# Layer norm with a residual add: 8-row tiles against 4-row tiles, with more and smaller buffers

## Chip, cores, metric

The kernel runs on one core of one Trainium2 chip. The metric is the device time of one execution in microseconds (us). The "span" of a profile is the profiled execution itself; it is about 2 us shorter than the device time (272.0 against 273.9 us in the profiled run of the kernel before).

## The reference

```python
# x, residual: (16, 1024, 512) float32; gamma, beta: (512,)
z = x + residual
mean = np.mean(z, axis=-1, keepdims=True)
var = np.var(z, axis=-1, keepdims=True)
return gamma * ((z - mean) / np.sqrt(var + eps)) + beta     # float32
```

There are 16,384 rows of 512 values. Each of the 128 partitions holds 128 consecutive rows, so "a row" below means one row on each of 128 partitions (256 KiB of each tensor), and there are 128 of them.

## The kernel before

The rows are cut into tiles: 14 of 8 rows, then 8 of 2 rows (the tail).

```python
R_MAIN = 8; R_TAIL = 2
n_tail = 2 * (R_MAIN // R_TAIL)
...
    R = R_MAIN if rem > n_tail * R_TAIL else R_TAIL
...
xz    = tile_pool(name="xz", bufs=3)      # x, later z       8 rows f32 each
rl    = tile_pool(name="rl", bufs=3)      # residual         8 rows f32 each
mids  = tile_pool(name="mids", bufs=2)    # ut, wt           8 rows bf16 each
outs  = tile_pool(name="outs", bufs=2)    # ot               8 rows f32 each
stats = tile_pool(name="stats", bufs=2)   # sums, ssq, m2, varn, stdv, rstd, cc

def emit_loads(i):                        # a 2-row tile takes a whole 8-row buffer
    zt = xz.tile([P, R_MAIN, D], f32, tag="zt")[:, :R]
    nc.sync.dma_start(out=zt, in_=x_v[:, r0 : r0 + R])
    rt = rl.tile([P, R_MAIN, D], f32, tag="rt")[:, :R]
    nc.sync.dma_start(out=rt, in_=r_v[:, r0 : r0 + R])
...
for i in range(n_t + 1):
    emit_loads(i + 3)
    emit_norm(i - 1)       # ACT: ut = z * rstd + cc, row by row           (L202)
    emit_sums_stt(i)       # DVE: z = x + r with its sum (L99); ACT: sum of squares (L106)
    emit_m2_stt(i)         # DVE: -sum^2/D                                 (L119)
    emit_fin(i - 1)        # DVE: wt = ut * gamma (L215), ot = wt + beta (L227); store (L231)
    emit_var_stt(i)        # DVE: varn (L131); ACT: sqrt                   (L135)
    emit_rstd_stt(i)       # DVE: reciprocal (L146), cc = -mean * rstd     (L148)
```

Loads are issued from the SP queue and stores from the GpSimd queue. A tile scheduler decides the final order on each engine, so the emission order is a hint. An x buffer is free again when ACT has normalized its tile; a residual buffer is free when DVE has added it.

## Time and profile before

| | before |
|---|---|
| device time, median of 4 runs | 274.05 us |
| moved by DMA | 101.26 MB |
| DVE busy / ACT busy | 197.2 us (72%) / 190.1 us (70%) |
| mean rate over the span | 372 GB/s |

This is the slice table of the page of the kernel before. The span is cut into 40 equal slices of 6.8 us; digits are tenths of busy time, the last line is what the DMA engines moved.

```profile
DVE  0166998896966969737888959839597758938752
ACT  0199879797929596881997989563968775554850
DMA  7998999999999999999999999999928567699623
GB/s 296 434 426 337 434 429 431 426 434 431 431 426 436 430 426 434 428 431 429 431 431 431 428 431 431 431 423 434 414 105 308 233 270 270 270 349 358 257 95 136
```

Up to slice 28 (about 197 us) the DMA engines move some 430 GB/s. The last 11 slices hold a quarter of the time at roughly half of that rate. The table by windows of the same trace looks closer (columns: window, its length, busy us and instructions of DVE, ACT and POOL, granted clock, DMA busy share, GB/s):

```profile
198.00:202.00 4.00, 4.00 (x4) 3.81 (x12) 0.00 (x0) 1.00 0.26 100
202.00:206.00 4.00, 4.00 (x8) 1.02 (x3) 0.53 (x1) 1.00 0.13 57
...
214.00:218.00 4.00, 4.00 (x3) 2.02 (x7) 0.00 (x0) 1.00 0.37 150
218.00:222.00 4.00, 3.03 (x11) 2.67 (x5) 0.53 (x1) 1.00 0.47 197
...
230.00:234.00 4.00, 4.00 (x4) 0.24 (x1) 0.58 (x2) 1.00 0.16 66
```

In these windows the DMA engines idle while DVE works on an 8-row tile. The waits of the load queue (who waited for what: us in total, times, longest us) say why nothing was loaded then:

```profile
SPq L73 <- ACT ut L202: 136.5, 14, 18.7
...
SPq L73 <- ACT stdv L135: 26.1, 4, 12.5
```

The queue stands until ACT has normalized an earlier tile, that is, until a buffer comes free. In the body this costs nothing, because enough loads are under way. At the end it does: this is the timeline around the last load of all (start us, duration us, engine, line, operation, count, idle time before it and what ended it).

```profile
251.92 1.50 ACT L202 ACTIVATE ut<-zt,cc,rstd 128x512 bf16<-128x512 f32 x2
...
253.45 0.33 SPq L73 DMA_DIRECT2D zt<-in_x_dram  x1
...
256.83 0.69 DVE L99 SCALAR_TENSOR_TENSOR zt<-zt,rt 128x512 f32<-128x512 f32 x1 [1.28 <-DMA zt<-in_x_dram]
```

The last load is issued only when the norm of an earlier tail tile ends, at 253.4 us. Its add begins at 256.8 us.

### The profile page before, as it was taken

What the parts mean: (1) busy time and instruction counts of PE and PEld (TensorE: products, weight loads), DVE (VectorE), ACT (ScalarE), POOL (GpSimd) and SP (SyncE); (2) the same over time, 40 slices, a digit from 0 to 9 for tenths busy, and PEclk for the clock granted to TensorE, in tenths of its full rate; (3) what the DMA queues carried; (4) which work ended last, traced back from release to release, by engine and by line L of the source; (5) the groups of instructions that cost most, each with busy time, mean ns of one, the idle gap of its engine ahead of it and who ended that gap; (6) DMA issues with size and microseconds to landing.
All of it is one profiled execution on the core that took longest, in us unless ns stands there. A gap on an engine that the chain in (4) does not pass through costs nothing.

```text
span 272.0 us, 1134 instructions
## 1 busy us (share of the span) xinstructions
DVE 197.2 (72%) x391; ACT 190.1 (70%) x408; POOL 12.0 (4%) x26
## 2 busy tenths in 40 slices
DVE  0166998896966969737888959839597758938752
ACT  0199879797929596881997989563968775554850
POOL 0000000000000000000000000000000000101010
DMA  7998999999999999999999999999928567699623
GB/s 296 434 426 337 434 429 431 426 434 431 431 426 436 430 426 434 428 431 429 431 431 431 428 431 431 431 423 434 414 105 308 233 270 270 270 349 358 257 95 136
DMA packets 9800, 101.26 MB, mean 372 GB/s; under 512 B 1088, under 2 KB 1088, under 8 KB 4416
## 3 DMA queue, kind: packets, MB, share of 16 engines
q1 hardware_dynamic: 6624, 67.64, 59.4%
q0 software_dynamic: 3168, 33.56, 30.1%
q14 instruction: 8, 0.07, 0.1%
HBM read 67.63 MB, written 33.55 MB: 372 GB/s over the span
## 4 chain that ended last, share of the span: by engine, by line
issue 49%; DMA 32%; ACT 8%; DVE 5%; POOL 3%; SPq 1%; POOLq 0%; DVEq 0%; ACTq 0%
DMA rt<-in_residual_dram 32%; ACT ut L202 7%; DVE ot L227 3%; POOL out_dram L231 3%; DVE zt L99 1%; ACT sq_junk L106 1%; DVE wt L215 1%; SPq L73 1%; POOLq L297 0%; SPq L77 0%; DVE varn L131 0%; POOLq L231 0%; DVEq L99 0%; ACTq L106 0%
## 5 line engine op out<-in xcount | busy, mean ns | idle before, releaser
L99 DVE SCALAR_TENSOR_TENSOR zt<-zt,rt 128x512 f32<-128x512 f32 x128 | 81.7, 683 | 34.3 <-DMA rt<-in_residual_dram 22.7
L202 ACT ACTIVATE ut<-zt,cc,rstd 128x512 bf16<-128x512 f32 x128 | 92.3, 800 | 16.2 <-DVE cc L148 16.2
L106 ACT ACTIVATE sq_junk<-zt 128x512 f32<-128x512 f32 x128 | 76.6, 599 | 22.5 <-DVE zt L99 14.1
L227 DVE TENSOR_TENSOR ot<-wt,beta_f 128x4096 f32<-128x4096 bf16 (+1 forms) x22 | 71.6, 3258 | 0.2
L215 DVE TENSOR_TENSOR wt<-ut,gamma_bf 128x4096 bf16<-128x4096 bf16 (+1 forms) x22 | 37.5, 1708 | 28.3 <-ACT ut L202 28.2
L135 ACT ACTIVATE stdv<-varn,eps_t 128x8 f32<-128x8 f32 (+1 forms) x22 | 6.4, 292 | 28.4 <-DVE varn L131 28.4
L106 ACT ACTIVATION_READ_ACCUMULATOR sq_junk<-zt 128x1 f32 x128 | 23.9, 187 | 0.0
L231 POOL DMA_DIRECT2D out_dram<-ot x22 | 11.8, 537 | 255.7 <-DVE varn L131 193.1
L99 DVE DVE_READ_ACCUMULATOR zt<-zt,rt 128x1 f32 x128 | 10.4, 81 | 0.0
L106 ACT ACT_TABLE_LOAD x1 | 1.3, 1283 | 8.0 <-DMA zt<-in_x_dram 8.0
L146 DVE RECIPROCAL rstd<-stdv 128x8 f32<-128x8 f32 (+1 forms) x22 | 4.0, 184 | 2.6 <-ACT stdv L135 2.6
L131 DVE TENSOR_TENSOR varn<-ssq,m 128x8 f32<-128x8 f32 (+1 forms) x22 | 3.4, 156 | 2.9 <-ACT sq_junk L106 2.8
L119 DVE SCALAR_TENSOR_TENSOR m<-sums 128x8 f32<-128x8 f32 (+1 forms) x22 | 3.6, 162 | 0.4
L148 DVE SCALAR_TENSOR_TENSOR cc<-sums,rstd 128x8 f32<-128x8 f32 (+1 forms) x22 | 3.5, 160 | 0.2
L135 ACT ACT_TABLE_LOAD x1 | 1.3, 1283 | 0.0
L244 DVE CAST beta_bf<-beta_f 128x512 bf16<-128x512 f32 x1 | 0.4, 427 | 0.4 <-DMA beta_f<-in_beta_dram 0.4
L246 DVE MEMSET eps_t<- 128x1 f32 x1 | 0.1, 59 | 0.8 <-PEq L283 0.8
L242 DVE CAST gamma_bf<-gamma_f 128x512 bf16<-128x512 f32 x1 | 0.4, 423 | 0.0
L283 POOL MEMSET const-float32-0.0<- 128x1 f32 x1 | 0.1, 99 | 0.2 <-issue 0.2
L283 POOL MEMSET const-bfloat16-1.0<- 128x1 bf16 x1 | 0.1, 102 | 0.0
L283 POOL MEMSET const-float32-1.0<- 128x1 f32 x1 | 0.1, 99 | 0.0
L283 POOL MEMSET const-uint8-127<- 128x1 uint8 x1 | 0.1, 99 | 0.0
## 6 DMA issues: line engine op xcount, KB each, us to landing
zt<-in_x_dram SPq DMA_DIRECT2D x14, 2048.0 KB, 14.7
rt<-in_residual_dram SPq DMA_DIRECT2D x14, 2048.0 KB, 21.9
out_dram<-ot POOLq DMA_DIRECT2D x14, 2048.0 KB, 13.9
rt<-in_residual_dram SPq DMA_DIRECT2D x8, 512.0 KB, 7.3
zt<-in_x_dram SPq DMA_DIRECT2D x8, 512.0 KB, 5.3
out_dram<-ot POOLq DMA_DIRECT2D x8, 512.0 KB, 3.0
gamma_f<-in_gamma_dram SPq DMA_DIRECT2D x1, 256.0 KB, 20.5
beta_f<-in_beta_dram SPq DMA_DIRECT2D x1, 256.0 KB, 21.9
```

Source lines behind the costliest of these rows:

```text
L73: nc.sync.dma_start(out=zt, in_=x_v[:, r0 : r0 + R])
L99: nc.vector.scalar_tensor_tensor(out=zt[:, j], in0=zt[:, j], scalar=0.0, in1=rt[:, j], op0=OP.add, op1=OP.add, accum_out=sums[:, j : j + 1],)
L106: nc.scalar.activation(out=sq_junk, in_=zt[:, j], func=AT.Square, accum_out=ssq[:, j : j + 1],)
L119: nc.vector.scalar_tensor_tensor(out=m2[:, :R], in0=s["sums"][:, :R], scalar=-inv_d, in1=s["sums"][:, :R], op0=OP.mult, op1=OP.mult,)
L131: nc.vector.tensor_tensor(out=varn[:, :R], in0=s["ssq"][:, :R], in1=s["m2"][:, :R], op=OP.add)
L135: nc.scalar.activation(out=stdv[:, :R], in_=varn[:, :R], func=AT.Sqrt, bias=eps_t, scale=inv_d)
L146: nc.vector.reciprocal(out=rstd[:, :R], in_=s["stdv"][:, :R])
L148: nc.vector.scalar_tensor_tensor(out=cc[:, :R], in0=s["sums"][:, :R], scalar=-inv_d, in1=rstd[:, :R], op0=OP.mult, op1=OP.mult,)
L202: nc.scalar.activation(out=ut[:, j], in_=s["zt"][:, j], func=AT.Identity, bias=s["cc"][:, j : j + 1], scale=s["rstd"][:, j : j + 1],)
L215: nc.vector.tensor_tensor(out=wt, in0=ut, in1=gamma_bf.unsqueeze(1).to_broadcast((P, R, D)), op=OP.mult,)
L227: nc.vector.tensor_tensor(out=ot[:, :R], in0=wt, in1=beta_f.unsqueeze(1).to_broadcast((P, R, D)), op=OP.add,)
L231: nc.gpsimd.dma_start(out=o_v[:, r0 : r0 + R], in_=ot[:, :R])
```

## The change

The intent is a finer pipeline: 4-row tiles, eight load buffers for each input (the same bytes per partition as four of the old ones), three instead of two middle and statistics buffers, four half-size output buffers, and a tail of 7 tiles of 2 rows and 2 of 1 row. Dead branches and an unused bf16 copy of beta go too.

```diff
+_R = 4
+_XB = 8
+_RB = 8
+_OB = 4
...
-        R = R_MAIN if rem > n_tail * R_TAIL else R_TAIL
+        R = _R if rem > 16 else (2 if rem > 2 else 1)
+        R = min(R, rem)
...
-    xz = ctx.enter_context(tc.tile_pool(name="xz", bufs=3))
-    rl = ctx.enter_context(tc.tile_pool(name="rl", bufs=3))
-    mids = ctx.enter_context(tc.tile_pool(name="mids", bufs=2))
-    outs = ctx.enter_context(tc.tile_pool(name="outs", bufs=2))
-    stats = ctx.enter_context(tc.tile_pool(name="stats", bufs=2))
+    xz = ctx.enter_context(tc.tile_pool(name="xz", bufs=_XB))
+    rl = ctx.enter_context(tc.tile_pool(name="rl", bufs=_RB))
+    mids = ctx.enter_context(tc.tile_pool(name="mids", bufs=3))
+    outs = ctx.enter_context(tc.tile_pool(name="outs", bufs=_OB))
+    stats = ctx.enter_context(tc.tile_pool(name="stats", bufs=3))
...   # every tile: [P, R_MAIN, D] -> [P, _R, D]; dead "bn", "dma" and cast branches removed
-    beta_bf = consts.tile([P, D], bf16)
-    nc.vector.tensor_copy(out=beta_bf, in_=beta_f)
...
     for i in range(n_t + 1):
-        emit_loads(i + 3)
+        for k in range(6):
+            emit_loads(i + 2 + k)
```

More of the change, by code (lines that the diff above doesn't have):

```diff
@@ L7 @@
 from concourse._compat import with_exitstack
-_ADD_MODE = "stt"
-_CAST_STORE = False
+_R = 4
+_XB = 8
+_RB = 8
+_OB = 4
+_CAST_R = False
+_STORE_Q = "pool"
 @with_exitstack
@@ L39 @@
     eps_f = float(eps)
-    R_MAIN = 8
-    R_TAIL = 2
-    n_tail = 2 * (R_MAIN // R_TAIL)
     n_rows = N // P
@@ L68, in emit_loads, with emit_sums @@
     def emit_loads(i):
-        if i >= n_t:
+        if i >= n_t or i in st:
             return
         r0, R = tiles[i]
-        zt = xz.tile([P, R_MAIN, D], f32, name=f"zt{i}", tag="zt")[:, :R]
+        zt = xz.tile([P, _R, D], f32, name=f"zt{i}", tag="zt")[:, :R]
         nc.sync.dma_start(out=zt, in_=x_v[:, r0 : r0 + R])
-        st[i] = dict(zt=zt)
-        if _ADD_MODE != "dma":
-            rt = rl.tile([P, R_MAIN, D], f32, name=f"rt{i}", tag="rt")[:, :R]
-            nc.sync.dma_start(out=rt, in_=r_v[:, r0 : r0 + R])
-            st[i]["rt"] = rt
-    def emit_accum(i):
-        if i >= n_t or i < 0 or _ADD_MODE != "dma":
-            return
-        r0, R = tiles[i]
-        nc.gpsimd.dma_start(
-            out=st[i]["zt"], in_=r_v[:, r0 : r0 + R],
-            accum_op=OP.add, max_dma_last_dim=1024,
-        )
-    sq_junk = junk.tile([P, D], f32, name="sq_junk") if _ADD_MODE != "dma" else None
-    def emit_sums_stt(i):
+        if _CAST_R:
+            rt = rl.tile([P, _R, D], bf16, name=f"rt{i}", tag="rt")[:, :R]
+            nc.gpsimd.dma_start(out=rt, in_=r_v[:, r0 : r0 + R])
+        else:
+            rt = rl.tile([P, _R, D], f32, name=f"rt{i}", tag="rt")[:, :R]
+            nc.sync.dma_start(out=rt, in_=r_v[:, r0 : r0 + R])
+        st[i] = dict(zt=zt, rt=rt)
+    sq_junk = junk.tile([P, D], f32, name="sq_junk")
+    def emit_sums(i):
         if i >= n_t or i < 0:
@@ L96, in emit_sums_stt @@
         zt, rt = s["zt"], s["rt"]
-        sums = stats.tile([P, R_MAIN], f32, name=f"sums{i}", tag="sums")
+        sums = stats.tile([P, _R], f32, name=f"sums{i}", tag="sums")
         for j in range(R):
@@ L103, in emit_sums_stt @@
             )
-        ssq = stats.tile([P, R_MAIN], f32, name=f"ssq{i}", tag="ssq")
+        ssq = stats.tile([P, _R], f32, name=f"ssq{i}", tag="ssq")
         for j in range(R):
@@ L111, in emit_sums_stt, with emit_m2 @@
         s["ssq"] = ssq
-    def emit_m2_stt(i):
+    def emit_m2(i):
         if i >= n_t or i < 0:
@@ L117, in emit_m2_stt @@
         r0, R = tiles[i]
-        m2 = stats.tile([P, R_MAIN], f32, name=f"m2{i}", tag="m2")
+        m2 = stats.tile([P, _R], f32, name=f"m2{i}", tag="m2")
         nc.vector.scalar_tensor_tensor(
@@ L123, in emit_m2_stt, with emit_var @@
         s["m2"] = m2
-    def emit_var_stt(i):
+    def emit_var(i):
         if i >= n_t or i < 0:
@@ L129, in emit_var_stt @@
         r0, R = tiles[i]
-        varn = stats.tile([P, R_MAIN], f32, name=f"varn{i}", tag="varn")
+        varn = stats.tile([P, _R], f32, name=f"varn{i}", tag="varn")
         nc.vector.tensor_tensor(
@@ L133, in emit_var_stt @@
         )
-        stdv = stats.tile([P, R_MAIN], f32, name=f"stdv{i}", tag="stdv")
+        stdv = stats.tile([P, _R], f32, name=f"stdv{i}", tag="stdv")
         nc.scalar.activation(
@@ L138, in emit_var_stt, with emit_rstd @@
         s["stdv"] = stdv
-    def emit_rstd_stt(i):
+    def emit_rstd(i):
         if i >= n_t or i < 0:
@@ L144, in emit_rstd_stt @@
         r0, R = tiles[i]
-        rstd = stats.tile([P, R_MAIN], f32, name=f"rstd{i}", tag="rstd")
+        rstd = stats.tile([P, _R], f32, name=f"rstd{i}", tag="rstd")
         nc.vector.reciprocal(out=rstd[:, :R], in_=s["stdv"][:, :R])
-        cc = stats.tile([P, R_MAIN], f32, name=f"cc{i}", tag="cc")
+        cc = stats.tile([P, _R], f32, name=f"cc{i}", tag="cc")
         nc.vector.scalar_tensor_tensor(
             out=cc[:, :R], in0=s["sums"][:, :R], scalar=-inv_d, in1=rstd[:, :R],
-            op0=OP.mult, op1=OP.mult,
-        )
-        s["rstd"] = rstd
-        s["cc"] = cc
-    def emit_stats_bn(i):
-        if i >= n_t or i < 0:
-            return
-        s = st[i]
-        r0, R = tiles[i]
-        zt = s["zt"]
-        bstats = stats.tile([P, R_MAIN, 6], f32, name=f"bs{i}", tag="bs")
-        for j in range(R):
-            nc.vector.bn_stats(out=bstats[:, j], in_=zt[:, j])
-        mv = stats.tile([P, R_MAIN, 2], f32, name=f"mv{i}", tag="mv")
-        for j in range(R):
-            nc.vector.bn_aggr(out=mv[:, j], in_=bstats[:, j])
-        s["mv"] = mv
-    def emit_sqrt_bn(i):
-        if i >= n_t or i < 0:
-            return
-        s = st[i]
-        r0, R = tiles[i]
-        stdv = stats.tile([P, R_MAIN], f32, name=f"stdv{i}", tag="stdv")
-        nc.scalar.activation(
-            out=stdv[:, :R], in_=s["mv"][:, :R, 1], func=AT.Sqrt, bias=eps_t, scale=1.0
-        )
-        s["stdv"] = stdv
-    def emit_rstd_bn(i):
-        if i >= n_t or i < 0:
-            return
-        s = st[i]
-        r0, R = tiles[i]
-        rstd = stats.tile([P, R_MAIN], f32, name=f"rstd{i}", tag="rstd")
-        nc.vector.reciprocal(out=rstd[:, :R], in_=s["stdv"][:, :R])
-        cc = stats.tile([P, R_MAIN], f32, name=f"cc{i}", tag="cc")
-        nc.vector.scalar_tensor_tensor(
-            out=cc[:, :R], in0=s["mv"][:, :R, 0], scalar=-1.0, in1=rstd[:, :R],
             op0=OP.mult, op1=OP.mult,
@@ L199, in emit_norm @@
         r0, R = tiles[i]
-        ut = mids.tile([P, R_MAIN, D], bf16, name=f"ut{i}", tag="ut")
+        ut = mids.tile([P, _R, D], bf16, name=f"ut{i}", tag="ut")
         for j in range(R):
@@ L213, in emit_fin @@
         ut = s["ut"][:, :R]
-        wt = mids.tile([P, R_MAIN, D], bf16, name=f"wt{i}", tag="wt")[:, :R]
+        wt = mids.tile([P, _R, D], bf16, name=f"wt{i}", tag="wt")[:, :R]
         nc.vector.tensor_tensor(
@@ L218, in emit_fin @@
         )
-        if _CAST_STORE:
-            ot = outs.tile([P, R_MAIN, D], bf16, name=f"ot{i}", tag="ot")
-            nc.vector.tensor_tensor(
-                out=ot[:, :R], in0=wt,
-                in1=beta_bf.unsqueeze(1).to_broadcast((P, R, D)), op=OP.add,
-            )
-        else:
-            ot = outs.tile([P, R_MAIN, D], f32, name=f"ot{i}", tag="ot")
-            nc.vector.tensor_tensor(
-                out=ot[:, :R], in0=wt,
-                in1=beta_f.unsqueeze(1).to_broadcast((P, R, D)), op=OP.add,
-            )
-        nc.gpsimd.dma_start(out=o_v[:, r0 : r0 + R], in_=ot[:, :R])
+        ot = outs.tile([P, _R, D], f32, name=f"ot{i}", tag="ot")
+        nc.vector.tensor_tensor(
+            out=ot[:, :R], in0=wt,
+            in1=beta_f.unsqueeze(1).to_broadcast((P, R, D)), op=OP.add,
+        )
+        eng = nc.scalar if _STORE_Q == "act" else nc.gpsimd
+        eng.dma_start(out=o_v[:, r0 : r0 + R], in_=ot[:, :R])
         del st[i]
@@ L242 @@
     nc.vector.tensor_copy(out=gamma_bf, in_=gamma_f)
-    beta_bf = consts.tile([P, D], bf16)
-    nc.vector.tensor_copy(out=beta_bf, in_=beta_f)
     eps_t = consts.tile([P, 1], f32)
     nc.vector.memset(eps_t, eps_f)
-    emit_accum(0)
-    emit_loads(2)
-    emit_accum(1)
     for i in range(n_t + 1):
-        emit_loads(i + 3)
+        for k in range(6):
+            emit_loads(i + 2 + k)
         emit_norm(i - 1)
-        if _ADD_MODE == "dma":
-            emit_stats_bn(i)
-            emit_fin(i - 1)
-            emit_accum(i + 2)
-            emit_sqrt_bn(i)
-            emit_rstd_bn(i)
-        else:
-            emit_sums_stt(i)
-            emit_m2_stt(i)
-            emit_fin(i - 1)
-            emit_var_stt(i)
-            emit_rstd_stt(i)
+        emit_sums(i)
+        emit_m2(i)
+        emit_fin(i - 1)
+        emit_var(i)
+        emit_rstd(i)
 _INS = ['x', 'residual', 'gamma', 'beta', 'eps']
```

## The prediction

> **What bounds the kernel now.** The program moves 101.26 MB (page, DMA packets). The slice table has 426 to 436 GB/s in nearly every slice from 27 to 197 us, DMA busy 9 tenths or more; the table by stage gives 431, 430, 430 GB/s in 40 to 80, 80 to 120, 120 to 160 us. So the body is bound by the DMA engines. DVE and ACT are 72% and 70% busy: near, but not the limit. At 430 GB/s all bytes would take an estimated 235 us; the span is 272.0. The difference is the tail: by stage some 83.9 MB have moved by 200 us, so the last 72 us move about 17.4 MB, which need 43 us even at the 406 GB/s that the tail's 4 KB packets reach when nothing starves them (1 us windows, 240 to 243 us). The windows at 202 to 204, 216 to 220 and 231 to 233 us move 0 bytes. Cause, from the waits of the load queue: it stands for a buffer (136.5 us on the norm L202, 26.1 on L135). Tail tiles have 2 rows but each holds one of three 8-row buffers, so 6 rows at most are in flight.
>
> **What the change does.**
> 1. 4-row tiles in 8+8 load buffers: 32 rows ahead in the body instead of 24, and 16 rows (all of the tail) instead of 6 in the tail. I expect the tail's zero-byte holes to go. Worth about 20 of the tail's 29 lost us; the rest is the last tile's chain.
> 2. First compute after 2 MB instead of 4 MB: first DVE add at about 7.5 us, not 12.85.
> 3. Packets of 8 KB, not 16 KB. From 430 GB/s at 16 KB and 406 at 4 KB I interpolate (fixed cost per packet) 422 GB/s: about +4 us over the body. Packets should rise from 9,800 to some 16,300. The Trainium skill, "DMA: Bandwidth & Descriptors", Rules for kernel authors, asks for at least 1 MiB per DMA; loads are now exactly 1 MiB in the body, 0.5 and 0.25 MiB in the tail. This trace's 0.5 MiB loads, queued back to back, still reach about 406.
> 4. 37 tiles instead of 22: 15 more sets of four small DVE operations (0.15 to 0.20 us each) and one sqrt (0.29): about +10 us DVE, +4 us ACT, and about 0.3 us of fixed cost for each further L215/L227 pair. Off the critical path while DMA bounds.
> 5. Removed: beta_bf cast (0.43 us), dead branches: nothing.
>
> **Is compute fast enough?** A 4-row tile takes 3.15 MB/422 = 7.45 us of DMA. Occupied DVE per tile: 4 x 0.61 + 0.5 x (2.29 + 4.42) + small ones = about 6.3 us; ACT 4 x 0.71 + 4 x 0.755 + 0.3 = 6.2. But the loop varn, sqrt, rstd, cc, norm, wt, ot, varn costs 0.97 + 2.9 + 1.2 + 2.2 = about 7.3 us when the order is good (as at 62 us), and 8.5 when adds and squares are placed in front of cc and norm (as at 94 us, 2.2 instead of 0.97). This is the main danger.
>
> **Sum.** Start 2 + body 209 + tail 31 + gamma and beta 2.5 + last chain 7 = 252 us. Range 246 to 264.
>
> **Right or wrong.** Right: no zero-byte slice before the last two; body slices near 420 GB/s; load-queue waits fall; most DVE idle time ends on loads. Wrong: body slices well under 415 with DVE waiting on L202 and ACT on L148 (the loop bounds; 265 to 280 us), or 8 KB packets cost more than 2%.
>
> Faster by over 2% (under 268.6): 0.87; within 2%: 0.09; slower: 0.04.

## The result

The changed kernel takes 256.18 us (median of 8 runs, 255.85 to 256.33); the kernel before, in the same rounds and the first ones, 273.93 us (13 runs, 273.53 to 274.61). The ratio is 0.935, 95% interval 0.9341 to 0.9359: faster by 6.5%. A ratio here is the mean time of one kernel's fast runs over that of the other's in the same rounds, so it is not quite the ratio of the medians. The output is correct.

The slice table of the changed kernel (slices of 6.3 us):

```profile
DVE  0488887889897897798877587898979597999972
ACT  0697769688878778669887478789697968789970
DMA  7999999999999999999999999999999999999543
GB/s 265 421 343 425 426 425 429 422 427 426 427 427 425 426 427 423 427 429 422 427 430 423 427 422 423 430 426 422 429 425 426 423 413 421 419 414 375 209 191 141
```

The DMA engines now stay full until about 232 us. The body runs at about 426 GB/s instead of 430. The windows of the end, in the columns of before:

```profile
198.00:202.00 4.00, 1.19 (x5) 4.00 (x7) 0.00 (x0) 1.00 1.03 430
202.00:206.00 4.00, 3.77 (x8) 3.90 (x10) 0.00 (x0) 1.00 1.00 415
...
230.00:234.00 4.00, 4.00 (x11) 3.94 (x12) 0.53 (x1) 1.00 0.85 353
234.00:238.00 4.00, 4.00 (x16) 3.70 (x8) 0.53 (x1) 1.00 0.70 281
```

The holes are gone, and at the end DVE is fully busy. The waits of the load queue:

```profile
SPq L81 <- DMA rt<-in_residual_dram: 100.2, 30, 4.9
SPq L75 <- DMA zt<-in_x_dram: 78.4, 30, 4.6
...
SPq L75 <- ACT ut L157: 5.7, 1, 5.7
```

It hardly waits for buffers any more: all its waits for an engine to release one come to 16 us, against 234 us before. It waits for its own earlier transfers: at the start of the trace it issues eight loads in a row, and the ninth only at 5.66 us, when the first has landed.

```profile
4.41 0.45 SPq L81 DMA_DIRECT2D rt<-in_residual_dram  x1
5.66 0.33 SPq L75 DMA_DIRECT2D zt<-in_x_dram  x1
```

So no more than eight loads were under way, four tiles, whatever the eight buffers per input would allow. (The trace shows the limit of eight; whether it comes from the chip or from how the program assigns its semaphores, it doesn't show.)

How far had each kernel come at a given time? I counted in the timelines of DVE how many rows had been added (L99 or L94) and how many finished (the instruction that writes ot had started):

| us | before: added / finished | 4-row tiles in the kernel before (b_R4, below) | changed |
|---|---|---|---|
| 198 | 106 / 88 | 106 / 96 | 107 / 96 |
| 220 | 115 / 104 | 116 / 108 | 117 / 108 |
| 231 | 116 / 112 | 120 / 114 | 124 / 114 |
| 240 | 120 / 114 | 124 / 120 | 127 / 122 |
| end of span | 272.0 | 259.9 | 253.9 |

The timeline merges like instructions, so rows must be counted with care: in the kernel before, the entry of 5.55 us below is one 8-row tile (4.4 us) and one 2-row tile (1.2 us), and the next tile follows only at 240.98 us.

```profile
228.10 5.55 DVE L227 TENSOR_TENSOR ot<-wt,beta_f 128x4096 f32<-128x4096 bf16 x2
...
240.98 1.20 DVE L227 TENSOR_TENSOR ot<-wt,beta_f 128x1024 f32<-128x1024 bf16 x1
```

At 240 us the kernel before is behind on both counts: 4 to 7 rows fewer added, 6 to 8 fewer finished. Of the added rows only 6 are unfinished, against 4 and 5 in the others: it has little loaded to work on. From there it needs 32 us for its last 14 rows, the kernel with 4-row tiles 20 us for 8, and the changed kernel 14 us for 6, some 2.3 to 2.5 us for each row in all three.

### The profile page after: what moved, and what is told of

It is laid out like the page before. It is cut to its first block, busy times and chain, and to the rows that moved or that the text cites. A ratio compares the mean times of both kernels' runs of the same rounds, so it can differ in the third digit from the quotient of the medians.

```text
span 253.9 us, 1320 instructions
## 1 busy us (share of the span) xinstructions
DVE 203.9 (80%) x480; ACT 192.2 (76%) x423; POOL 20.0 (8%) x41
## 2 busy tenths in 40 slices
DMA packets 16154, 101.28 MB, mean 399 GB/s; under 512 B 1808, under 2 KB 1808, under 8 KB 5392
## 4 chain that ended last, share of the span: by engine, by line
DMA 84%; DVE 6%; issue 5%; ACT 2%; POOL 1%; SPq 0%; POOLq 0%; DVEq 0%; ACTq 0%
DMA rt<-in_residual_dram 84%; DVE zt L94 2%; ACT ut L157 2%; DVE wt L170 2%; DVE ot L175 2%; POOL out_dram L180 1%; SPq L75 0%; POOLq L234 0%; DVE cc L143 0%; DVE varn L126 0%; DVE rstd L141 0%; DVE m L114 0%; DVEq L94 0%; ACTq L101 0%; POOLq L180 0%
## 5 line engine op out<-in xcount | busy, mean ns | idle before, releaser
L157 ACT ACTIVATE ut<-zt,cc,rstd 128x512 bf16<-128x512 f32 x128 | 93.3, 801 | 25.3 <-DVE cc L143 25.2
L94 DVE SCALAR_TENSOR_TENSOR zt<-zt,rt 128x512 f32<-128x512 f32 x128 | 82.7, 685 | 33.8 <-DMA rt<-in_residual_dram 33.6
L175 DVE TENSOR_TENSOR ot<-wt,beta_f 128x2048 f32<-128x2048 bf16 (+2 forms) x37 | 74.0, 2001 | 0.2
L170 DVE TENSOR_TENSOR wt<-ut,gamma_bf 128x2048 bf16<-128x2048 bf16 (+2 forms) x37 | 39.8, 1077 | 6.0 <-ACT ut L157 5.9
L180 POOL DMA_DIRECT2D out_dram<-ot x37 | 19.8, 536 | 229.5 <-DVE varn L126 152.5
L130 ACT ACTIVATE stdv<-varn,eps_t 128x4 f32<-128x4 f32 (+2 forms) x37 | 10.6, 287 | 11.2 <-DVE varn L126 11.2
L94 DVE DVE_READ_ACCUMULATOR zt<-zt,rt 128x1 f32 x128 | 10.5, 82 | 0.0
L141 DVE RECIPROCAL rstd<-stdv 128x4 f32<-128x4 f32 (+2 forms) x37 | 6.2, 168 | 2.2 <-ACT stdv L130 2.2
L114 DVE SCALAR_TENSOR_TENSOR m<-sums 128x4 f32<-128x4 f32 (+2 forms) x37 | 5.8, 159 | 0.8
L126 DVE TENSOR_TENSOR varn<-ssq,m 128x4 f32<-128x4 f32 (+2 forms) x37 | 5.6, 151 | 1.1 <-ACT sq_junk L101 1.0
L143 DVE SCALAR_TENSOR_TENSOR cc<-sums,rstd 128x4 f32<-128x4 f32 (+2 forms) x37 | 5.8, 156 | 0.1
```

The source lines that it names most:

```text
L94: nc.vector.scalar_tensor_tensor(out=zt[:, j], in0=zt[:, j], scalar=0.0, in1=rt[:, j], op0=OP.add, op1=OP.add, accum_out=sums[:, j : j + 1],)
L114: nc.vector.scalar_tensor_tensor(out=m2[:, :R], in0=s["sums"][:, :R], scalar=-inv_d, in1=s["sums"][:, :R], op0=OP.mult, op1=OP.mult,)
L126: nc.vector.tensor_tensor(out=varn[:, :R], in0=s["ssq"][:, :R], in1=s["m2"][:, :R], op=OP.add)
L130: nc.scalar.activation(out=stdv[:, :R], in_=varn[:, :R], func=AT.Sqrt, bias=eps_t, scale=inv_d)
L141: nc.vector.reciprocal(out=rstd[:, :R], in_=s["stdv"][:, :R])
L143: nc.vector.scalar_tensor_tensor(out=cc[:, :R], in0=s["sums"][:, :R], scalar=-inv_d, in1=rstd[:, :R], op0=OP.mult, op1=OP.mult,)
```

## The experiments

Twelve kernels ran; all outputs but those of the three copies without compute are correct. "Before" in the same rounds was 273.7 to 274.1 us. The edits are shown shortened.

### Transfers alone (d_only8, d_only4, d_only2)

The compute is taken out; the output is wrong. Both inputs are loaded and the x tile is stored, with 12 MiB of load buffers (3 + 3, 6 + 6 or 12 + 12 buffers).

```diff
-    for i in range(n_t + 1):   # all the stages
+    for i in range(n_t):
+        for k in range(3):     # 6, 12 for the smaller tiles
+            emit_loads(i + k)
+        nc.gpsimd.dma_start(out=o_v[:, r0 : r0 + R], in_=st[i]["zt"])
```

> No compute at all (output wrong on purpose): both inputs are loaded and the x tile is stored, 8-row tiles, 16 KB packets, 2 MiB per transfer. If the bodies of both kernels are bound by the DMA engines alone, the slices show about 430 GB/s as in the kernel before and the time is about 101.3 MB / 430 GB/s + 5 us of start and end = 240 us. Rival (compute or its waits hold the body back): clearly less, under 232 us.

> The same with 4-row tiles, 8 KB packets, 1 MiB per transfer. Theory (small cost per packet, as the body of the changed kernel shows 426 GB/s): 242 to 244 us. Rival (transfers of 1 MiB reach only about 78% of peak, as the single-transfer table of the skill could be read): about 300 us.

> The same with 2-row tiles, 4 KB packets, 0.5 MiB per transfer. Theory: 406 to 415 GB/s, 248 to 254 us. If 4 KB packets cost nothing: 240 us.

Measured: 244.65, 246.07 and 252.01 us (two runs each). The first is about 5 us and the second 2 us above what was expected; the third lies in its range. The rates are as expected or better, so the time at the start and the end was put too low. The slices of d_only8, d_only4 and d_only2:

```profile
GB/s 270 408 386 432 428 387 427 432 432 432 429 432 427 429 429 432 432 432 432 429 429 429 432 429 432 432 432 432 432 432 429 432 432 432 432 432 432 432 408 165
```

```profile
GB/s 253 368 425 426 398 427 427 427 426 427 429 429 427 427 427 429 425 427 429 425 425 427 429 425 426 427 429 427 427 423 427 427 426 425 427 425 427 426 429 165
```

```profile
GB/s 268 316 421 420 419 420 420 420 420 421 421 418 419 420 420 419 419 418 419 420 418 420 418 419 419 419 419 419 419 419 418 420 420 419 419 418 420 419 409 89
```

Without compute the rate is the same as in the bodies of the two full kernels, 430 to 432 GB/s with 16 KB packets and 426 to 427 with 8 KB ones. So the bodies are bound by the DMA engines. The finer transfers cost 1.4 us in all; 4 KB packets (about 420 GB/s) would cost 7.4 us. The Trainium skill, "DMA: Bandwidth & Descriptors", lists 341 GB/s for a 1 MB transfer (section Measured, the table that the expectation of d_only4 means). In a queue with others behind it, the 1 MiB transfer here does not show that: 427 GB/s. The kernel before stands 29.5 us above its floor (274.1 - 244.65) and the changed one 10.1 us above its own (256.2 - 246.07). That difference is what the change is about.

### Own buffers for the tail of the kernel before (b_tailbufs)

```diff
+    tl = ctx.enter_context(tc.tile_pool(name="tl", bufs=4))
...
-        zt = xz.tile([P, R_MAIN, D], f32, tag="zt")[:, :R]
+        zt = tl.tile([P, R_TAIL, D], f32, tag="zs") if R == R_TAIL else xz.tile([P, R_MAIN, D], f32, tag="zt")
...     # rt the same
```

> The kernel before with one change: the 2-row tail tiles get load buffers of their own, 4 + 4 of 4 KB per partition, instead of one of the three 8-row buffers each. Theory (the tail starves because a 2-row tile holds an 8-row buffer): most of the gain comes from here, 256 to 261 us, the windows without a byte between 202 and 233 us go. Rival (the gain comes from the early start, the finer body or the deeper body prefetch): 268 us or more.

Measured: 270.02 us, ratio 0.9856 (0.9833 to 0.9878). The gain is there, but it is 4.1 us, within 2% of the kernel before. The number lies in the rival's range (268 us or more). But the holes are not gone, as a window of this kernel shows:

```profile
214.00:221.00 7.00, 6.96 (x12) 3.69 (x10) 0.53 (x1) 1.00 0.09 37
```

The timeline says why. The fifth tail tile's load waits for the first tail tile's buffer, and is issued at 226.85 us, when ACT has normalized it:

```profile
219.68 7.14 ACT L209 ACTIVATE ut<-zt,cc,rstd 128x512 bf16<-128x512 f32 x10
...
226.85 0.33 SPq L77 DMA_DIRECT2D zt<-in_x_dram  x1
```

Four small buffers hold 8 rows of the tail; three large ones held 6. The experiment moved the limit by only 2 rows, so it was too weak a test of the theory it was meant for, and its number doesn't speak for the rival either.

### 4-row tiles in the kernel before (b_R4)

```diff
-    R_MAIN = 8
+    R_MAIN = 4
-    n_tail = 2 * (R_MAIN // R_TAIL)
+    n_tail = 8
-... name="xz", bufs=3 / name="rl", bufs=3
+... name="xz", bufs=6 / name="rl", bufs=6      # the same bytes
```

> The kernel before with body tiles of 4 rows instead of 8 and 6 + 6 load buffers instead of 3 + 3 (the same bytes), still 8 tail tiles of 2 rows; middle, output and statistics buffers stay at 2, the emission order stays. Revised theory (the time after the last body load is the drain of compute that runs 2 to 3 tiles behind the loads, so the tile's size sets it, not the depth of the buffers): 261 to 265 us, as the changed kernel with small pools (262.0). Rival (the gain needs the changed kernel's earlier emission of loads or its 8 buffers): 268 us or more.

Measured: 261.79 us, ratio 0.9555 (0.954 to 0.9571), 12 us of the 17.9. The number falls where the revised theory put it. The compute is further along, as it said: 120 rows are finished at 240 us, and 114 in the kernel before. But the loads are earlier too, and the theory gave the buffers no part: six of them now hold 12 rows of the tail instead of 6, and the last load is issued at 228.4 us and not at 253.4 us. So this run alone doesn't separate the tile's size from the room for the tail; the table in the next section does so for the loads. Set beside b_tailbufs: 6, 8 and 12 tail rows in buffers gave 274.1, 270.0 and 261.8 us, about 2 us for each row. These three points fit the buffers as the cause; a kernel with 8-row body tiles and room for all 16 tail rows, which would have settled the time too, did not run.

### Fewer load buffers (a_buf6, a_buf4)

The changed kernel with one constant pair altered: `_XB = _RB = 6`, or 4.

> The changed kernel with 6 + 6 load buffers. Theory (4 tiles in flight plus two in work): 256.2 within 1 us. Rival A (each additional buffer counts): between the result with 4 and with 8.

> The changed kernel with 4 + 4 load buffers instead of 8 + 8. Theory (only 8 loads of this queue are ever in flight, which is 4 tiles, so the load queue waits for its own earlier transfers and not for buffers; but tiles in work hold buffers too): some buffer waits come back, 256 to 262 us. Rival A (depth of 8 tiles is what gives the gain): back at 268 us or more. Rival B (depth is without any effect): 256.2 within 0.5 us.

Measured: 257.24 us (0.9387) with 6 and 265.11 us (0.9684) with 4. The last two buffers are worth about 1 us, the two before them 7.9 us. With 6 the result is just outside the theory's 1 us and fits its rival; with 4 it lies between the theory's range (256 to 262 us) and rival A's (268 us or more). With 4, the tail holds 8 rows again, and slices without full DMA come back from 204 us on:

```profile
GB/s 270 409 357 425 426 425 426 427 422 426 428 426 428 425 421 430 425 427 426 424 430 425 424 424 422 415 367 430 426 427 425 276 299 349 321 372 323 252 169 151
```

The body is untouched but for one slice (367). So the deep prefetch matters at the end and hardly in the body.

Set beside the earlier runs, these two also answer for the loads what b_R4 left open. The traces give for each kernel when the last load was issued and when it landed (us; "room" is the number of tail rows that the buffers hold):

| kernel | body tile | room | last load issued / landed | from there to the end of the span |
|---|---|---|---|---|
| before | 8 rows | 6 | 253.4 / 256.7 | 15.3 |
| b_tailbufs | 8 rows | 8 | 241.9 / 247.0 | 21.2 |
| a_buf4 | 4 rows | 8 | 245.1 / 248.0 | 15.1 |
| b_R4 | 4 rows | 12 | 228.4 / 236.5 | 23.4 |
| a_buf6 | 4 rows | 12 | 231.1 / 236.7 | 18.4 |
| changed | 4 rows | 15 | 224.3 / 236.7 | 17.2 |

With the same room the last load lands at the same time within 1 us, with 8-row tiles (b_tailbufs) as with 4-row tiles (a_buf4); with more room it lands up to 20 us earlier. So the room for the tail, and not the tile's size, decides when the loads are done. (The a_ kernels also have the larger middle, statistics and output buffers.) The time after that is the drain; it is longest where the loads come early but the other pools stay small (b_tailbufs, b_R4).

### Small middle, statistics and output buffers (a_small_pools)

```diff
-_OB = 4
+_OB = 2
-... name="mids", bufs=3 / name="stats", bufs=3
+... name="mids", bufs=2 / name="stats", bufs=2
```

> The changed kernel with the statistics and middle buffers at 2 instead of 3 and the output buffers at 2 instead of 4, as the kernel before has them; all else as changed. Theory (three sets of statistics let the adds of later tiles be queued ahead of the finish of earlier ones, so that 4 tiles are unfinished when the last loads come, 19 us from the last landing to the end): fewer adds ahead, the end shrinks by some us, 250 to 255 us. Rival (the additional buffers are needed for overlap): slower, 258 us or more.

Measured: 262.02 us, ratio 0.9564 (0.9545 to 0.9584). This is 5.8 us slower than the changed kernel, and the same as b_R4. My theory fell; the rival holds. With small pools, then, the other differences from b_R4 (eight load buffers, earlier emission, 1-row tiles) bring nothing. The loads are as early as in the changed kernel, but the adds lag: at 231 us this kernel has added 120 rows against 124, with 114 finished in both. Waits of its engines:

```profile
ACT ut L157 <- DVE cc L143: 43.7, 33, 3.0
...
DVE ot L175 <- DMA out_dram<-ot: 2.4, 1, 2.4
```

In the changed kernel the first of these is 25.2 us in 22 waits, and the second does not occur. From 240 us on DVE does 8.5 us of work in 10 us here and, between 230 and 240 us, 8.0; the changed kernel has 10.0 there. Which of the three pools counts was not taken apart.

### The tail's grain (a_tail4, a_tail32)

```diff
-        R = _R if rem > 16 else (2 if rem > 2 else 1)
+        R = _R                                            # a_tail4
+        R = _R if rem > 32 else (2 if rem > 2 else 1)     # a_tail32
```

> The changed kernel without small tiles at the end, 4 rows throughout. Theory (the end is bound by unfinished compute, and a smaller last tile shortens the last chain): 4 to 8 us slower, 260 to 264 us. Rival (small tiles cost as much in DVE work and packets as they save): 256 within 1 us.

> The changed kernel with 2-row tiles for the last 32 rows instead of the last 16. Revised theory (unfinished rows behind the loads set the end; 2-row tiles leave fewer rows unfinished): 250 to 254 us. Rival (the end is bound by DVE work alone, and 2-row tiles cost more of it, about 0.1 us per row): 257 to 260 us.

Measured: 263.74 us (0.9627) without small tiles, as the theory had it, and 257.78 us (0.9409) with twice as many rows in them, where the theory fell. The small tail is worth 7.6 us, and the 16 rows of it were enough. More small tiles lose 1.6 us: DVE is busy 205.5 us instead of 203.9 us, and at 240 us it had finished 120 rows, not 122. The rival of that run, that DVE work counts at the end, fits.

### Another order on DVE (c_dep_body)

In the changed kernel's body the scheduler's order on DVE is: adds of tile i, wt of i-2, reciprocal of i-1, ot of i-2, cc of i-1, varn of i. A tile is thus finished two tiles after its adds. One ordering edge brings that down to one:

```diff
-        emit_sums(i)
+        if 0 < i < 28:
+            with tc.issue_after(st[i - 1]["cc_ins"].ins):   # adds of i behind cc of i-1
+                emit_sums(i)
+        else:
+            emit_sums(i)
```

> The changed kernel with one forced order: for the 4-row tiles, DVE may add tile i+1 only after it has issued cc of tile i, so that a tile is finished one tile earlier (after the adds of the next tile instead of the second next). Theory (the scheduler's order keeps one tile of 4 rows more unfinished, worth about 5 us at the end): 250 to 254 us. Rival (the order costs more DVE idle time in the body than it saves: an estimated 7.35 us of compute against 7.4 us of DMA for a tile): 257 to 265 us with body slices under 420 GB/s.

Measured: 257.54 us, ratio 0.94 (0.9385 to 0.9415), 1.4 us slower than the changed kernel. Two successive passes of the loop in its timeline:

```profile
101.42 0.16 DVE L126 TENSOR_TENSOR varn<-ssq,m 128x4 f32<-128x4 f32 x1
...
108.79 0.16 DVE L126 TENSOR_TENSOR varn<-ssq,m 128x4 f32<-128x4 f32 x1
```

The loop takes 7.37 us, where the prediction had estimated 7.3, and a tile's 3.15 MB at 427 GB/s also take 7.37 us: compute and DMA just balance, and the body stays at 423 to 431 GB/s. So the order did what it should; at 198 us 4 more rows were finished (100 against 96), but 3 fewer were added (104 against 107). At 210 us the lead was gone (104 and 104). What used it up was not taken apart. The theory fell; the time lies in the rival's range (257 to 265 us), but the slow body slices that the rival named are not there. An earlier finish in the body did not shorten the end.

### Three of the last additions on GpSimd (c_pool_end)

```diff
-        nc.vector.tensor_tensor(out=ot[:, :R], in0=wt, ...)
+        fe = nc.gpsimd if i in (27, 29, 31) else nc.vector
+        fe.tensor_tensor(out=ot[:, :R], in0=wt, ...)
```

> The changed kernel, but the last addition (ot) of tiles 27, 29 and 31 is done by GpSimd instead of DVE: 4.7 us of DVE work less in a stretch in which DVE is busy 95% and more. The scheduler also reorders the end of the program, which the comparison can't separate. Theory (DVE throughput bounds the drain after the loads): 250 to 253 us, faster than the changed kernel by 3 us or more. Rival (the drain is bound by ACT, which is about as busy, by the chain of dependences, or GpSimd's adds are slow and hold up the stores): 255 us or more.

Measured: 262.18 us, ratio 0.9583 (0.9567 to 0.9599), 6 us slower than the changed kernel. The timeline:

```profile
223.82 4.08 POOL L176 TENSOR_TENSOR ot<-wt,beta_f 128x2048 f32<-128x2048 bf16 x1 [3.55 <-DVE wt L170]
...
223.92 4.53 DVE L170 TENSOR_TENSOR wt<-ut,gamma_bf 128x1024 bf16<-128x1024 bf16 x1 [0.19 <-ACT ut L157]
...
232.14 2.13 POOL L176 TENSOR_TENSOR ot<-wt,beta_f 128x1024 f32<-128x1024 bf16 x1 [1.03 <-DVE rstd L141]
...
232.16 2.12 DVE L143 SCALAR_TENSOR_TENSOR cc<-sums,rstd 128x2 f32<-128x2 f32 x1
```

The DVE instruction that began during a GpSimd addition lasted until that addition ended, or half a microsecond longer: cc took 2.12 us instead of 0.16, wt 4.53 us instead of 0.69. The three stalls (3.8 + 2.0 + 2.0 us) exceed the 4.7 us saved by 3 us; the other 3 us are not explained. The Trainium skill, "SBUF — State Buffer", section "SBUF: two separate sides", says that a GpSimd instruction that reads SBUF and a DVE instruction with two SBUF inputs share a port pair which the first of them holds for its whole instruction; this trace agrees. So the run says nothing about what a less loaded DVE would be worth; that the drain is bound by DVE work rests on its busy share (10.0 of 10 us between 230 and 240 us) and on a_tail32 alone. ACT is at 9.5 of 10 us there, so relieving DVE alone could not have brought much.

No experiment beat the changed kernel.

## Why the prediction was right, and where it was off

The time (252 predicted, 246 to 264 as the range, 256.2 measured) and the direction were right. That the sum came so near is in part luck: errors in its terms made up for each other. Point by point:

- **"The body is bound by the DMA engines."** Right. The copies without compute run at the same rates as the bodies, and the changed kernel holds 422 to 430 GB/s from slice 3 to slice 31. Most of DVE's idle time before the adds ends on a load (33.6 us).
- **"Tail tiles hold 8-row buffers, so 6 rows at most are in flight", worth about 20 us.** The mechanism is supported: 6, 8 and 12 tail rows in buffers gave 274.1, 270.0 and 261.8 us. The term was mis-sized. With 12 rows the last load does land 20 us earlier (236.5 and not 256.7 us), but the drain behind it is 8 us longer (23.4 and not 15.3 us), so this step brought about 12 us (b_R4), and one isolated attempt at it only 4.1 us.
- **"32 rows ahead in the body instead of 24."** This did not happen: at most eight loads, 16 rows, were under way at a time. It cost nothing, since the body ran at the same rate with 4 buffers per input.
- **Not in the prediction at all: the middle, statistics and output buffers.** They are in the diff, and I costed nothing for them. They brought 5.8 us (a_small_pools). The total came out near because this missing term made up for the mis-sized one.
- **"First add at about 7.5 us."** It was at 8.22 us. What the earlier start is worth by itself was not tested; with a DMA-bound body it should be nothing, which is an argument and not a measurement.
- **"8 KB packets: 422 GB/s, +4 us."** Direction right, size too large: 426 to 427 GB/s and 1.4 us. My interpolation took 406 GB/s for 4 KB packets from a stretch of the old tail; undisturbed they reach about 420. Packets: 16,154, predicted 16,300.
- **"+10 us DVE, +4 us ACT", off the critical path.** DVE rose by 6.7 us (197.2 to 203.9), ACT by 2.1.
- **"The loop costs 7.3 us in a good order, 8.5 in a bad one: the main danger."** 7.37 us was measured with the good order forced. The danger did not come: the scheduler chose a third order, which finishes a tile later and waits less.
- **"Last chain 7."** This is the step that failed most. The sum put 7 us behind the last byte. In the trace the chain of waits has the residual load of the second-last tile land at 235.07 us, and the span ends at 253.9: 18.8 us (17.2 us after the last load of all). The loads come in earlier than the sum had it, because stores lag behind them; then DVE has about 12 rows to finish and DMA is only half busy. So it is wrong to charge all bytes first and one last tile's chain after them: at the end the limit changes from DMA to compute.

## What to carry to other kernels

In a kernel bound by DMA, look at when the DMA engines first go idle near the end: what the compute still has to do from there is the time to be had. Count, for the tail, how many rows the buffers can hold before the first tail tile gives its buffer back, since small tiles in large buffers waste the prefetch just where it is needed. Small buffers for statistics and results look harmless in a body that waits for DMA, but here they cost 5.8 us at the end, and a change of depth there should be costed like any other.

## What the Trainium skill lacked or had wrong

- "DMA: Bandwidth & Descriptors", section Measured, gives 341 GB/s for one 1 MB transfer and asks in its rules for 1 MiB or more. It has no table by packet size for loads and stores queued back to back: here 2 MiB transfers with 16 KB packets ran at about 432 GB/s, 1 MiB with 8 KB at 427, and 0.5 MiB with 4 KB at 420, loads and stores mixed.
- "DMA: Bandwidth & Descriptors", Specifications, names about 358 GB/s as the HBM limit of a core. On this core alone the body ran at 426 to 432 GB/s for some 200 us. (The page says under Measured that each core gets about 358 GB/s when both cores of a pair stream, so the row holds for that case only.)
- "Perfetto Trace Analysis", section Optimizing Scalar/DVE Operations, says that moving work from DVE to GpSimd might not help because of the shared port. It gives no number: here three such moves saved 4.7 us of DVE work, stalled DVE for 7.8 us and cost 6 us in all.
- No page that I read says that a stalled DVE instruction is shown as busy for the whole stall (cc: 2.12 us instead of 0.16), so that the busy share hides it.
- No page that I read has the limit of eight loads under way that the load queue of the changed kernel shows (ninth issue at 5.66 us, as the first lands).
